# A hybrid attention and convolution block on one core: score maxima one step later, the second norm's factor in one tile, and a last row block in two halves

## The chip, the core and the metric

The kernel runs on one core of one Trainium2 chip. A core has TensorE (matmuls; the profile calls it PE, its weight loads PEld), VectorE (DVE), ScalarE (ACT), GpSimd (POOL) and SyncE (SP), each with an instruction stream of its own that runs in order. The metric is the device time of one execution in microseconds (us), as the median of several runs. A profiled execution gives the trace: its span is the time from the first to the last instruction, and its own device time is a little longer.

## The reference

One layer on 256 tokens of width 2048, everything in float32:

```python
xn = rms_norm(h, norm1_g)
q, k, v, ga, gg = split(xn @ w_in)            # 4 heads, 2 score maps each, d = 128
q, k = rope(rms_norm(q)), rope(rms_norm(k))
p = softmax(q @ k.T * scale, masked by chunks of 64)   # for both maps
att = rms_norm((p[0] - lam * p[1]) @ v) * (1 - lambda_init)
u = silu(layer_norm(causal_depthwise_conv(ga * sigmoid(gg))))
h = h + concat(att, u) @ w_out
hn = rms_norm(h, norm2_g)
h = h + (silu(hn @ w_gate) * (hn @ w_up)) @ w_down     # hidden width 5632
```

## The kernel before

The tokens are two row blocks of 128 (`NM = 2`, index `m`). Every float32 weight tile is split on the chip into a rounded part (`whi`, cast on ScalarE at L325) and a remainder (`wlo`, subtracted on VectorE at L334, or made by an accumulating DMA); a product is then three fp32r matmuls: data-high by weight-high, data-low by weight-high (L364 and L365 in the projections, L1066 and L1067 in the feed-forward part), data-high by weight-low (L370, L1072).

The projections run as chunks of two 128-row slices of a weight against 512 columns: eight matmuls in a first half, four in a second (`multiply`, L340 on). Everything else is written as Python generators that run beside the chunks: `resume()`, called after each half chunk, lets every running generator go on to its next `yield`, and what it issues then stands at that place in each engine's stream. So `lag(n)` puts the next step n half chunks later. This, and nothing at run time, sets the order. On VectorE the taps of the depthwise convolution (L553, `y`) fill in between, as many per chunk as a running credit of time allows (`run_side`).

Attention, per head (`attend_scores`): TensorE makes the scores (`ps_s`, L692), VectorE masks them and takes the row maxima (L700 to L704, `nmx`), ScalarE the exponentials (L714, `pr`), VectorE the combined weights (L728, `wt`), TensorE transposes these (L736 to L738, `ps_wt`), ScalarE copies them out (L741). Per head again (`attend_values`): TensorE makes the output (`ps_o`, L762), ScalarE sums squares, GpSimd makes the norm's factor (L769, L770, `ro`), ScalarE scales (L774, `att`), TensorE transposes (L782, `ps_at`), ScalarE and VectorE split the result (L786 `mahi`, L789 `malo`). Heads 0 and 1 reach their scores near 162 us, heads 2 and 3 near 211 us, when the values of heads 0 and 1 are also on their way.

After the output projection, `out_done` sums the squares of each row block of `h` (L462) into `ss2[m]`. For the last quarter it reduces them and makes the factor `rstd2[m]` with `rsqrt_mean` (L222 and L223, on GpSimd: scale and add, then a power of -0.5), once for each row block. `make_forms` spreads these factors along rows: ScalarE writes `rep` (L953), TensorE transposes it (`ps_r`, L957), ScalarE copies it to `rb` (L960).

The feed-forward part uses sums of quarter matrices (seven products where eight blocks would be multiplied, PSUM banks `q0` to `q7`; `Q1` to `QX` are their numbers). Plain chunks are of kind "g" or "u" (`multiply_two`); a "u" chunk adds into bank Q3 for row block 0 and bank QX for row block 1. The last chunk of the program runs row block 0 whole, then row block 1 whole. `down_whole` then adds bank and residual (`hend[m]`, already holding the other terms) on VectorE in halves of 256 columns (L1220), and SP stores each half as it is ready (L1221). An earlier store of the block before leaves on GpSimd's queue (L1202).

Of the kernel before, what the change touches and what calls it, by code (L numbers as in the profile page):

```python
# [18 lines left out]
P = 128  # L19
D = 2048  # L20
# [107 lines left out]
def tile_block(  # L128
# [554 lines left out]
    def attend_scores(hd):  # L683
        scs = []
        yield
        yield from room(2, 2)
        for m in range(NM):
            L = (m + 1) * P
            sc = aux_ps.tile([P, 2, S], F32, tag="aux", name="ps_s")
            for c in range(2):  # L690
                g = 2 * hd + c
                pe.matmul(sc[:, c, :L], qkT["q"][:, g, m * P : (m + 1) * P], qkT["k"][:, g, :L],  # L692
                          start=True, stop=True)
            scs.append(sc)
        yield from lag(2)
        nmxs, fs, prs, sms = [], [], [], []
        for m in range(NM):
            L = (m + 1) * P
            sc = scs[m]
            dve.memset(sc[:CHUNK, :, L - CHUNK : L], MASKED)  # L700
            nmx = small.tile([P, 2], F32, tag="nmx", name="nmx")
            dve.tensor_reduce(nmx, sc[:, :, :L], AX.X, ALU.max, negate=True)
            f = fqs[hd // 2, m][:, hd % 2 * 2 : hd % 2 * 2 + 2]
            dve.tensor_tensor(nmx, nmx, f, ALU.mult)  # L704
            nmxs.append(nmx)
            fs.append(f)
        spend(0.1)
        yield from lag(3)
        for m in range(NM):
            L = (m + 1) * P  # L710
            pr = pre.tile([P, 2, S], F32, tag="pr", name="pr", bufs=4)
            sm = small.tile([P, 2], F32, tag="sm", name="sm")
            for c in range(2):
                act.activation(pr[:, c, :L], scs[m][:, c, :L], AF.Exp, bias=nmxs[m][:, c : c + 1],  # L714
                               scale=fs[m][:, c : c + 1], accum_out=sm[:, c : c + 1])
            prs.append(pr)
            sms.append(sm)
        held[0] -= 2
        yield from lag(2)
        wts = []  # L720
        for m in range(NM):
            L = (m + 1) * P
            r = small.tile([P, 1], F32, tag="r", name="r")
            c = small.tile([P, 1], F32, tag="a1", name="c")
            dve.reciprocal(r, sms[m][:, 1:2])
            dve.scalar_tensor_tensor(c, sms[m][:, 0:1], neg_lam, r, ALU.mult, ALU.mult)
            wt = pre.tile([P, S], F32, tag="wt", name="wt", bufs=4)
            dve.scalar_tensor_tensor(wt[:, :L], prs[m][:, 1, :L], c, prs[m][:, 0, :L], ALU.mult, ALU.add)  # L728
            pool.tensor_scalar(eps_s[:, hd, m : m + 1], sms[m][:, 0:1], sms[m][:, 0:1], EPS, ALU.mult, ALU.mult)
            wts.append(wt)  # L730
        spend(0.3)
        spend(0.4)
        yield from lag(4)
        yield from room(1)
        pt = aux_ps.tile([P, 3, P], F32, tag="aux", name="ps_wt")
        pe.transpose(pt[:, 0, :], wts[0][:, :P], ident)  # L736
        pe.transpose(pt[:, 1, :], wts[1][:, :P], ident)
        pe.transpose(pt[:, 2, :], wts[1][:, P:], ident)  # L738

        wT = qkT["q"][:, 2 * hd : 2 * hd + 2, :].rearrange("p g s -> p (g s)")[:, : 3 * P].rearrange("p (k s) -> p k s", k=3)  # L740
        act.copy(wT, pt)  # L741
        wTs[hd] = wT
# [51 lines left out]

    hn = []
    ss2 = [const.tile([P, 4], F32, tag=f"ss2_{m}", name=f"ss2_{m}") for m in range(NM)]
    rstd2 = [const.tile([P, 1], F32, tag=f"rstd2_{m}", name=f"rstd2_{m}") for m in range(NM)]

    def out_done(n, ps):
        cs = slice(n * N, (n + 1) * N)  # L800
        for m in range(NM):
            dve.tensor_tensor(h[m][:, cs], h[m][:, cs], ps[m], ALU.add)
        if n == 2:
            held[0] -= NM
        yield
        for t in range(0, N // P, 2):
            k = n * (N // P) + t
            yield from room(1)
            pt = aux_ps.tile([P, 2, S], F32, tag="aux", name="ps_h")
            for i in range(2):  # L810
                for m in range(NM):
                    pe.transpose(pt[:, i, m * P : (m + 1) * P], h[m][:, (k + i) * P : (k + i + 1) * P], ident)
            if k % HK == 0:
                hn.append(early.tile([P, HK, S], F32, tag="wb", name="hn"))
            rows = hn[k // HK][:, k % HK : k % HK + 2, :]
            for i in range(2):
                act.activation(rows[:, i, :], pt[:, i, :], AF.Copy, scale=col("g2", k + i))
            hi, lo = lhs_two("h", k)
            act.copy(hi, rows)
            dve.tensor_tensor(lo, rows, hi.bitcast(F32), ALU.subtract)  # L820
            for i in range(2):
                hT[k + i] = (hi[:, i, :], lo[:, i, :])
            yield
        for m in range(NM):
            square_sum(h[m][:, cs], ss2[m][:, n : n + 1])
            pool.dma_start(out=hd[m][:, cs], in_=h[m][:, cs])
        if n == D // N - 1:
            yield
            for m in range(NM):
                ss = small.tile([P, 1], F32, tag="ssh", name="ssh")  # L830
                dve.tensor_reduce(ss, ss2[m], AX.X, ALU.add)
                rsqrt_mean(rstd2[m], ss, D, EPS)
            yield
            yield
            prestack.close()
            ffn["pool"] = ctx.enter_context(tc.tile_pool(name="ffn", bufs=1))
            start(make_forms())
# [216 lines left out]
    def multiply_two(c):  # L1054
        hi, lo = c["hi"], c["lo"]
        qs = (Q3, QX) if c["kind"] == "u" else (Q2, Q4)
        xs = []
        for k in c["ks"]:
            while (x := c["plain"](k)) is None:
                resume()  # L1060
            xs.append(x)

        def first_half(m):
            ms = slice(m * P, (m + 1) * P)
            ps = sum_bank(c, qs[m])
            pe.matmul(ps, xs[i][0][:, ms], hi[:, i, :], start=i == 0 and bool(c["first"].get(qs[m])), stop=False)  # L1066
            pe.matmul(ps, xs[i][1][:, ms], hi[:, i, :], start=False, stop=False)  # L1067

        def second_half(m):
            ms = slice(m * P, (m + 1) * P)  # L1070
            for i in range(2):
                pe.matmul(sum_bank(c, qs[m]), xs[i][0][:, ms], lo[:, i, :], start=False,  # L1072
                          stop=i == 1 and bool(c["last"].get(qs[m])))

        if c is chunks[-1]:

            for m in range(NM):
                for i in range(2):
                    first_half(m)
                second_half(m)  # L1080
        else:
            for i in range(2):
                for m in range(NM):
                    first_half(m)
            resume()
            for m in range(NM):
                second_half(m)
        resume()
        if c["done"]:
            start(c["done"](c["sums"]))  # L1090
# [118 lines left out]
    def down_whole(g, n, q, end):  # L1209
        while "us" not in end:  # L1210
            yield
        us = end["us"]
        for m, i in enumerate((Q3, QX)):
            if not at_end(g, n):
                dve.tensor_tensor(us[m], q[i], us[m], ALU.add)
                continue
            w = N // 2
            for a in range(0, N, w):
                hs = hend[m][:, N + a : N + a + w]
                dve.tensor_tensor(hs, hs, q[i][:, a : a + w], ALU.add)  # L1220
                sp.dma_start(out=out[m * P : (m + 1) * P, (n + 1) * N + a : (n + 1) * N + a + w], in_=hs)  # L1221
        if not at_end(g, n):
            if FGROUPS[g] > 3:
                yield from lag(HD_LAG)
            for m in range(NM):
                pool.dma_start(out=hd[m][:, (n + 1) * N : (n + 2) * N], in_=us[m], accum_op=ALU.add)
        if g == len(FGROUPS) - 1 and not at_end(g, n):
            fetch_end()

            yield from lag(6)  # L1230
            for m in range(NM):
                cs = slice(n * N, (n + 2) * N)
                pool.dma_start(out=out[m * P : (m + 1) * P, cs], in_=hd[m][:, cs])
# [18 lines left out]
    for g, nb in enumerate(FGROUPS):  # L1252
# [7 lines left out]
            chunks[-1]["prompt"] = True  # L1260
        down_pass(g, j0, nb)
        j0 += nb

    near_pair = lambda t: any(c.get("kind") == "s" for c in chunks[t : t + HI_AHEAD + 1])
    lead = lambda t: (1, 1) if t < OPENING else (HI_AHEAD, LO_AHEAD) if near_pair(t) else (AHEAD, AHEAD)
# [46 lines left out]
```

## Time and profile before

| | |
|---|---|
| median of 3 runs | 1038.59 us (1038.37 to 1038.63) |
| profiled execution, device time | 1038.44 us |
| its span | 1036.7 us |
| granted TensorE clock | 1.00 |
| TensorE busy | 99% of the span |
| VectorE / ScalarE / GpSimd busy | 89% / 62% / 11% |
| last matmul ends | about 1032.6 us |

In a timeline a row gives the start in us, the duration in us, the engine, the source line, the operation, what it writes and reads, and in brackets how long its engine stood idle before it and for whom. `x4` means four such instructions merged into one row, whose duration then runs from the first one's start to the last one's end. Matmuls overlap: the next one starts before the row of the one before it ends, so distances are taken between starts. In a row of the waits stand the engine, the tile and line that waited, the one waited for, and then the total in us, the number of times and the longest. The windows view cuts the span into stretches and gives each engine's busy time in each.

### The profile page before, as it was taken

To read this page: it belongs to the slowest core of one execution; us is meant where nothing else is said; L and a number is where in the kernel's file an instruction comes from. 1 tells how busy PE (TensorE), PEld (TensorE's weight loads), DVE (VectorE), ACT (ScalarE), POOL (GpSimd) and SP (SyncE) were. 2 spreads that over 40 slices of the span, in tenths; PEclk is the share of its full clock that TensorE was granted. 3 is DMA by queue.
4 is the path that set the end of the run, shared out by engine and by line. 5 is a ranking of instruction groups with operands and counts; after the bars stand their busy time and mean duration, and the time that the engine had idled before them with its cause. 6 is when DMAs were issued, how large, how long until landed. Compare 5 with 4: busy or idle time off the path is not lost.

```text
span 1036.7 us, 13003 instructions
## 1 busy us (share of the span) xinstructions
PE 1028.9 (99%) x4639; PEld 848.7 (82%) x4639; DVE 926.5 (89%) x1125; ACT 638.3 (62%) x780; POOL 110.8 (11%) x149
## 2 busy tenths in 40 slices
PE   9999999999999999999999999999999999999998
PEld 7888888878888788888888888888888888888886
DVE  7899999989766599999999898989999989889887
ACT  7554657655666565777666556667757556667452
POOL 0130112111000100110102011101001111010010
PEclk9999999999999999999999999999999999999999
DMA  9657654553547677987989799879798979897773
GB/s 351 213 181 279 214 174 142 192 174 127 186 158 235 187 247 232 285 255 217 260 250 266 262 252 273 261 228 260 230 269 250 295 197 284 245 261 232 217 220 102
DMA packets 115664, 237.59 MB, mean 229 GB/s; under 512 B 7696, under 2 KB 8848, under 8 KB 115344
## 3 DMA queue, kind: packets, MB, share of 16 engines
q1 hardware_dynamic: 104864, 203.71, 58.7%
q0 software_dynamic: 10592, 33.04, 16.5%
q8 instruction: 36, 0.59, 0.2%
q14 instruction: 28, 0.23, 0.1%
q10 hardware_dynamic: 144, 0.03, 0.0%
HBM read 204.24 MB, written 9.44 MB: 206 GB/s over the span
## 4 chain that ended last, share of the span: by engine, by line
PE 63%; DVE 2%; issue 1%; ACT 0%; DVEq 0%
PE q L1066 11%; PE q L1067 11%; PE q L1072 11%; PE q L1047 9%; PE q L1045 9%; PE q L1046 9%; PE ps_a L870 1%; PE acc L370 1%; PE acc L364 1%; PE acc L365 1%; DVE wlo L334 1%; DVE wlt L1028 0%; DVE wt L1018 0%; DVE wt L1019 0%; ACT wh L1024 0%
## 5 line engine op out<-in xcount | busy, mean ns | idle before, releaser
L325 ACT CAST whi<-raw 128x1024 fp32r<-128x1024 f32 (+1 forms) x257 | 266.4, 1047 | 151.4 <-PE acc L365 82.0
L334 DVE TENSOR_TENSOR wlo<-raw,whi 128x1024 fp32r<-128x1024 f32 (+1 forms) x211 | 254.4, 1217 | 37.5 <-ACT whi L325 37.3
L1024 ACT CAST wh<-wt 128x2048 fp32r<-128x2048 f32 x60 | 114.9, 1915 | 108.3 <-DVE wt L1020 108.2
L1028 DVE TENSOR_TENSOR wlt<-wt,wh 128x2048 fp32r<-128x2048 f32 x60 | 137.5, 2291 | 19.5 <-ACT wh L1024 19.4
L364 PE MATMUL acc<-whi,xhi 128*128 128x512 f32 x320 | 127.2, 397 | 0.9 <-ACT whi L325 0.9
L365 PE MATMUL acc<-whi,xlo 128*128 128x512 f32 x320 | 125.3, 392 | 0.0
L1066 PE MATMUL q<-whi,chi 128*128 128x512 f32 x320 | 125.3, 391 | 0.0
L1067 PE MATMUL q<-whi,clo 128*128 128x512 f32 x320 | 124.6, 389 | 0.0
L1045 PE MATMUL q<-wh,fhi 128*128 128x512 f32 x280 | 109.9, 392 | 0.0
L1046 PE MATMUL q<-wh,flo 128*128 128x512 f32 x280 | 109.0, 389 | 0.0
L1027 DVE TENSOR_TENSOR wlb<-wb,wh 128x1536 fp32r<-128x1536 f32 x60 | 105.1, 1752 | 1.1 <-ACT wh L1021 1.1
L553 DVE SCALAR_TENSOR_TENSOR y<-upad,cw,y 128x256 f32<-128x256 f32 x240 | 101.9, 481 | 2.2 <-ACT y L546 2.2
L329 POOL DMA_DIRECT2D wlo<-raw x46 | 40.2, 875 | 507.9 <-ACT wlo L328 244.6
L1021 ACT CAST wh<-wb 128x1536 fp32r<-128x1536 f32 x60 | 88.4, 1473 | 0.0
L370 PE MATMUL acc<-wlo,xhi 128*128 128x512 f32 x320 | 87.4, 394 | 0.0
L1072 PE MATMUL q<-wlo,chi 128*128 128x512 f32 x320 | 85.6, 389 | 0.0
L1066 PE MATMUL q<-whi,ahi 128*128 128x512 f32 x192 | 74.9, 390 | 0.0
L1067 PE MATMUL q<-whi,alo 128*128 128x512 f32 x192 | 74.8, 389 | 0.0
L1018 DVE TENSOR_TENSOR wt<-wb 128x1024 f32<-128x1024 f32 x60 | 73.1, 1219 | 0.0
L364 PEld LDWEIGHTS acc<-whi,xhi 128*128 128x128 f32 x320 | 60.4, 189 | 14.3 <-ACT whi L325 1.7
L365 PEld LDWEIGHTS acc<-whi,xlo 128*128 128x128 f32 x320 | 60.4, 189 | 12.6
L1072 PEld LDWEIGHTS q<-wlo,chi 128*128 128x128 f32 x320 | 59.9, 188 | 12.8 <-DMA wlo<-raw 0.2
(245 smaller groups left out, 1833.9 us busy)
## 6 DMA issues: line engine op xcount, KB each, us to landing
raw<-in_w_in_dram SPq DMA_DIRECT2D x79, 512.0 KB, 4.6
raw<-in_w_gate_dram SPq DMA_DIRECT2D x48, 512.0 KB, 5.2
raw<-in_w_up_dram SPq DMA_DIRECT2D x48, 512.0 KB, 5.3
raw<-in_w_down_dram SPq DMA_DIRECT2D x48, 512.0 KB, 6.8
wlo<-raw POOLq DMA_DIRECT2D x46, 512.0 KB, 7.2
wb<-in_w_up_dram SPq DMA_DIRECT2D x40, 512.0 KB, 4.4
wb<-in_w_gate_dram SPq DMA_DIRECT2D x40, 512.0 KB, 5.5
wb<-in_w_down_dram SPq DMA_DIRECT2D x40, 512.0 KB, 6.0
```

The source lines that it names most:

```text
L325: act.copy(c["hi"], c["raw"])
L334: dve.tensor_tensor(c["lo"], c["raw"], c["hi"].bitcast(F32), ALU.subtract)
L364: pe.matmul(ps[m], xhi[:, ms], hi[:, j, :], start=c["first"] and j == 0, stop=False)
L365: pe.matmul(ps[m], xlo[:, ms], hi[:, j, :], start=False, stop=False)
L1024: act.copy(c["hi"][:, :SUMMED], c["t"])
L1027: dve.tensor_tensor(lob, c["b"][:, 1:], c["hi"][:, SUMMED:].bitcast(F32), ALU.subtract)
L1028: dve.tensor_tensor(lot, c["t"], c["hi"][:, :SUMMED].bitcast(F32), ALU.subtract)
L1045: pe.matmul(ps, hi, c["hi"][:, w], start=bool(first), stop=False)
L1046: pe.matmul(ps, lo, c["hi"][:, w], start=False, stop=False)
L1066: pe.matmul(ps, xs[i][0][:, ms], hi[:, i, :], start=i == 0 and bool(c["first"].get(qs[m])), stop=False)
L1067: pe.matmul(ps, xs[i][1][:, ms], hi[:, i, :], start=False, stop=False)
L1072: pe.matmul(sum_bank(c, qs[m]), xs[i][0][:, ms], lo[:, i, :], start=False, stop=i == 1 and bool(c["last"].get(qs[m])))
```

## The change

Three separate edits. First, the step of `attend_scores` that masks the scores and takes their maxima is queued three half chunks after the scores instead of two; all later steps of that head follow it. Second, the reduced sums of squares and the factor of the second norm become one tile of 128x2 for both row blocks, so `rsqrt_mean` is called once. Third, in the last chunk of the program row block 1 no longer adds into bank QX: bank QX is closed one chunk earlier and added to `hend[1]` by a new generator, `last_row_but_one`, and the last chunk's share of row block 1 goes, 256 columns at a time, into two fresh PSUM tiles (`qe`); the very last store is issued by ScalarE.

```diff
-        yield from lag(2)
+        yield from lag(3)
         nmxs, fs, prs, sms = [], [], [], []
...
-    rstd2 = [const.tile([P, 1], F32, tag=f"rstd2_{m}", name=f"rstd2_{m}") for m in range(NM)]
+    rstd2s = const.tile([P, NM], F32, tag="rstd2", name="rstd2")
+    rstd2 = [rstd2s[:, m : m + 1] for m in range(NM)]
...
+            ss = small.tile([P, NM], F32, tag="ssh", name="ssh")
             for m in range(NM):
-                ss = small.tile([P, 1], F32, tag="ssh", name="ssh")
-                dve.tensor_reduce(ss, ss2[m], AX.X, ALU.add)
-                rsqrt_mean(rstd2[m], ss, D, EPS)
+                dve.tensor_reduce(ss[:, m : m + 1], ss2[m], AX.X, ALU.add)
+            rsqrt_mean(rstd2s, ss, D, EPS)
...
         if c is chunks[-1]:
-            for m in range(NM):
+            for i in range(2):
+                first_half(0)
+            second_half(0)
+            c["sums"]["ends"] = []
+            for a in range(0, N, N // 2):
+                cs = slice(a, a + N // 2)
+                ps = acc_ps.tile([P, N], F32, tag="acc", name=f"qe{a}")[:, : N // 2]
                 for i in range(2):
-                    first_half(m)
-                second_half(m)
+                    xhi, xlo = (x[:, P:] for x in xs[i])
+                    pe.matmul(ps, xhi, hi[:, i, cs], start=i == 0, stop=False)
+                    pe.matmul(ps, xlo, hi[:, i, cs], start=False, stop=False)
+                for i in range(2):
+                    pe.matmul(ps, xs[i][0][:, P:], lo[:, i, cs], start=False, stop=i == 1)
+                c["sums"]["ends"].append(ps)
...
-                dve.tensor_tensor(hs, hs, q[i][:, a : a + w], ALU.add)
-                sp.dma_start(out=out[m * P : (m + 1) * P, (n + 1) * N + a : (n + 1) * N + a + w], in_=hs)
+                dve.tensor_tensor(hs, hs, q["ends"][a // w] if m else q[i][:, a : a + w], ALU.add)
+                (act if m and a else sp).dma_start(
+                    out=out[m * P : (m + 1) * P, (n + 1) * N + a : (n + 1) * N + a + w], in_=hs)
...
+    def last_row_but_one(q):
+        yield
+        dve.tensor_tensor(hend[1][:, N:], hend[1][:, N:], q[QX], ALU.add)
+    before_last = [c for c in chunks if c.get("kind") == "u"][-2]
+    before_last["last"][QX] = True
+    before_last["done"] = lambda q: last_row_but_one(q)
```

ScalarE's stream where heads 0 and 1 are scaled (`att`) and head 3's exponentials are taken (`pr`); the lines with a sign are those that moved:

```order
 L462 ACTIVATE junk,sso<-ps_o 128x256 x4
 L325 CAST whi<-raw 128x1024
+L774 ACTIVATE att<-ps_o,ro 128x256 x2
 L714 ACTIVATE pr,sm<-ps_s,nmx,fq 128x128 x2
 L714 ACTIVATE pr,sm<-ps_s,nmx,fq 128x256 x2
-L774 ACTIVATE att<-ps_o,ro 128x256 x2
 L786 ACTIVATE mahi<-ps_at,cols 128x256 x2
 L774 ACTIVATE att<-ps_o,ro 128x256 x2
 L325 CAST whi<-raw 128x1024
```

Head 0's scaling now stands ahead of head 3's exponentials, and these stand between it and head 1's scaling.

TensorE's stream a chunk later, before:

```order
L365 MATMUL acc<-whi,xlo_242 128x512
L736 MATMUL ps_wt<-ident,wt 128x128
L737 MATMUL ps_wt<-ident,wt 128x128
L738 MATMUL ps_wt<-ident,wt 128x128
L782 MATMUL ps_at<-ident,att 128x128 x4
L370 MATMUL acc<-wlo,xhi_241 128x512 x4
L364 MATMUL acc<-whi,xhi_265 128x512
```

and now:

```order
L365 MATMUL acc<-whi,xlo_241 128x512
L782 MATMUL ps_at<-ident,att 128x128 x4
L370 MATMUL acc<-wlo,xhi_240 128x512 x4
L736 MATMUL ps_wt<-ident,wt 128x128
L737 MATMUL ps_wt<-ident,wt 128x128
L738 MATMUL ps_wt<-ident,wt 128x128
L364 MATMUL acc<-whi,xhi_264 128x512
```

The transposes of head 2's weights have moved behind the second half of the chunk; the transposes of head 1's output come straight after its first half. The other three heads' weight transposes move past one second half in the same way.

The end of VectorE's stream, before:

```order
L1206 TENSOR_TENSOR hend<-hend,sum_8739 128x512
L1220 TENSOR_TENSOR hend<-hend,q_8680 128x256 x2
L1220 TENSOR_TENSOR hend<-hend,q_8729 128x256 x2
```

and now, where L1217 is the old L1206, L1231 the old L1220 and L1278 the new generator:

```order
L1217 TENSOR_TENSOR hend<-hend,sum_8734 128x512
L1278 TENSOR_TENSOR hend<-hend,q_8724 128x512
L1231 TENSOR_TENSOR hend<-hend,q_8675 128x256 x2
L1231 TENSOR_TENSOR hend<-hend,qe_8786 128x256
L1231 TENSOR_TENSOR hend<-hend,qe_8793 128x256
```

One sum of 512 columns is added, and the last two sums read a tile each instead of the two halves of one bank.

More of the change, by code (lines that the diff above doesn't have):

```diff
@@ L1262, in tile_block @@
         j0 += nb
+    def last_row_but_one(q):
+        yield
+        dve.tensor_tensor(hend[1][:, N:], hend[1][:, N:], q[QX], ALU.add)
+    before_last = [c for c in chunks if c.get("kind") == "u"][-2]
+    assert before_last["done"] is None
+    before_last["last"][QX] = True
+    before_last["done"] = lambda q: last_row_but_one(q)
     near_pair = lambda t: any(c.get("kind") == "s" for c in chunks[t : t + HI_AHEAD + 1])
```

## The prediction

> **What bounds the kernel now.** I read the page first (span, busy times), then the waits of TensorE alone, then the timeline at the three places that the diff touches.
>
> ```profile
> span 1036.7 us, 13003 instructions
> PE 1028.9 (99%) x4639; PEld 848.7 (82%) x4639; DVE 926.5 (89%) x1125; ACT 638.3 (62%) x780; POOL 110.8 (11%) x149
> ```
>
> TensorE is busy for all but 7.8 us. So a change that takes no matmul away can win only what TensorE idles, and the stretch after its last matmul. The waits of TensorE itself (us in total, times, longest) show where that is:
>
> ```profile
> PE ps_at L782 <- ACT att L774: 0.8, 1, 0.8
> PE ps_r L957 <- ACT rep L953: 0.3, 1, 0.3
> ```
>
> These are two places, both in the change: the transposes of the attention output (`ps_at`) and of the second norm's factor (`ps_r`). A matmul's row reaches past the start of the next, so the rows understate what is lost; I take each stall from start to start below. The third place is the end, where the chain leaves TensorE for VectorE and the stores.
>
> **Part one, the maxima a half chunk later.** The stall, on TensorE, and the same sequence without a wait 26 us later:
>
> ```profile
> 229.35 1.07 PE L370 MATMUL acc<-wlo,xhi 128*128 128x512 f32 x4
> 231.18 0.91 PE L782 MATMUL ps_at<-ident,att 128*128 128x128 f32 x4 [0.77 <-ACT att L774]
> 231.84 0.48 PE L364 MATMUL acc<-whi,xhi 128*128 128x512 f32 x1
> ...
> 256.65 1.07 PE L370 MATMUL acc<-wlo,mahi 128*128 128x512 f32 x4
> 257.56 0.60 PE L782 MATMUL ps_at<-ident,att 128*128 128x128 f32 x4
> 257.92 0.48 PE L364 MATMUL acc<-whi,mahi 128*128 128x512 f32 x1
> ```
>
> Undisturbed, the matmul behind the transposes starts 257.92 - 256.65 = 1.27 us after the `L370` group; here it took 231.84 - 229.35 = 2.49. The stall is 1.22 us. ScalarE shows why:
>
> ```profile
> 228.68 0.46 ACT L714 ACTIVATE pr<-ps_s,nmx,fq 128x128 f32<-128x128 f32 x1
> ...
> 230.64 0.85 ACT L774 ACTIVATE att<-ps_o,ro 128x256 f32<-128x256 f32 x2
> 232.13 0.84 ACT L786 ACTIVATE mahi<-ps_at,cols 128x256 fp32r<-128x256 f32 x2 [0.64 <-PE ps_at L782]
> 232.85 0.84 ACT L774 ACTIVATE att<-ps_o,ro 128x256 f32<-128x256 f32 x2
> ```
>
> Head 0's scaling (`L774`) stands behind head 3's exponentials (`L714`), which hold ScalarE for 230.64 - 228.68 = 1.96 us. The new order puts the scaling first. Its factor is there in time: the second of two such powers on GpSimd, head 1's, started at 228.19, so head 0's was done before.
>
> ```profile
> 228.19 0.70 POOL L770 TENSOR_TENSOR ro<-sso,neghalf 128x2 f32<-128x2 f32 x1
> ```
>
> So head 0's scaling starts at 228.68 instead of 230.64, the transposes find their input, and TensorE goes on at 229.35 + 1.27 = 230.62.
>
> Not all of that stays. The exponentials now stand ahead of head 1's scaling. A pair on ScalarE takes 0.72 us (232.13 to 232.85): head 0's scaling from 228.68, exponentials from 229.40, `mahi` from 231.36, head 1's scaling from 232.08. Before, `L364` started 231.84 - 230.64 = 1.20 us after the scaling that it waited for; so TensorE gets past head 1's transposes at 233.28. It would be ready for that earlier:
>
> ```profile
> 233.78 0.27 PE L736 MATMUL ps_wt<-ident,wt 128*128 128x128 f32 x1
> ...
> 234.11 0.60 PE L782 MATMUL ps_at<-ident,att 128*128 128x128 f32 x4
> 234.47 1.17 PE L370 MATMUL acc<-wlo,xhi 128*128 128x512 f32 x4
> 235.47 0.39 PE L364 MATMUL acc<-whi,xhi 128*128 128x512 f32 x1
> ```
>
> Eight matmuls take 233.78 - 231.84 = 1.94 us, the transposes 0.36, so 230.62 + 1.94 + 0.36 = 232.92. The stall returns as 0.36 us, since head 2's weight transposes (`L736`, 0.33 us), which stood between and covered it, have moved behind the `L370` group. That separate batch also costs a changeover: `L370` to `L364` took 1.00 us behind transposes and 0.91 without (256.65 to 257.56), so 0.09. Part one is worth 1.22 - 0.36 - 0.09 = 0.77 us. From both sides: 1.22 if nothing returns; a loss if the lateness of the maxima reaches TensorE elsewhere (a rival below).
>
> What else is queued behind the moved maxima? On VectorE three taps and a `wlo` subtraction now go ahead of them; that `wlo` waits for a cast:
>
> ```profile
> 213.13 0.17 DVE L700 MEMSET ps_s<- 64x128 f32 x1
> 215.47 1.27 DVE L553 SCALAR_TENSOR_TENSOR y<-upad,cw,y 128x256 f32<-128x256 f32 x3
> 214.65 1.05 ACT L325 CAST whi<-raw 128x1024 fp32r<-128x1024 f32 x1 [3.02 <-PE acc L365]
> 228.81 1.22 DVE L334 TENSOR_TENSOR wlo<-raw,whi 128x1024 fp32r<-128x1024 f32 x1 [1.58 <-ACT whi L325]
> ```
>
> From 213.13, where head 2's maxima began, the taps' 1.27 us bring VectorE to 214.4, the cast ends at 215.7, and everything behind runs up to 1.3 us late, until the pause of 1.58 us before 228.81 absorbs it. The weight transposes that need the maxima also move later, by the `L370` group's 0.91 us. I price this at nothing; without that cover it is the fourth rival.
>
> **Part two, the norm's factor in one tile.** Two POOL operations on 128x2 replace four on 128x1:
>
> ```profile
> 351.70 1.15 POOL L222 TENSOR_SCALAR rsq<-ssh 128x1 f32<-128x1 f32 x1 [7.38 <-DVE ssh L831]
> 352.93 0.57 POOL L223 TENSOR_TENSOR rstd<-rsq,neghalf 128x1 f32<-128x1 f32 x1
> 354.46 0.69 ACT L953 ACTIVATE rep<-ident,rstd 128x128 f32<-128x128 f32 x2 [3.23 <-POOL rstd L223]
> 354.21 0.39 PE L365 MATMUL acc<-whi,hlo 128*128 128x512 f32 x1
> 354.91 0.62 PE L957 MATMUL ps_r<-ident,rep 128*128 128x128 f32 x2 [0.32 <-ACT rep L953]
> 355.29 1.17 PE L370 MATMUL acc<-wlo,hhi 128*128 128x512 f32 x4
> ```
>
> A 512-column matmul takes 0.227 us from start to start (four in the 0.91 above), so TensorE was free at 354.44; a 128-column transpose takes 0.11 (233.78 to 234.11 for three). Unstalled, `L370` would start at 354.44 + 0.22 = 354.66; it started at 355.29. The stall is 0.63 us. Now the power runs once, on 128x2, for 0.70 us (the `L770` row): ready at 352.93 + 0.70 = 353.63, both `rep` done by 353.67 + 0.69 = 354.36, before TensorE asks at 354.44. Worth 0.63; at worst nothing: the first factor was ready at 353.5, and both `rep` waited for the second, up to 354.46, which is one operation with the first now. The first POOL operation, 1.15 us, I leave as it is.
>
> **Part three, the end.** The last row block ran in six 512-column matmuls, then two VectorE halves, then two stores on SP:
>
> ```profile
> 1031.98 0.61 PE L1072 MATMUL q<-wlo,ahi 128*128 128x512 f32 x2
> 1032.63 0.42 DVE hend L1220
> 1033.08 0.81 SPq L1221 DMA_DIRECT2D out_dram<-hend  x2
> L1221 SPq DMA_DIRECT2D out_dram<-hend x4: 332/360/385, 1031.7 to 1033.5; - x4
> DMA to landing us min/median/max: 1.9/1.9/1.9
> ```
>
> The last store was issued at 1033.5, 0.9 us after TensorE's end at 1032.6: behind both halves and the other store. Now only one half is behind the last matmul: 0.02 to its start, 0.42 for it (the chain's step), and 0.03 to the issue (1033.05 to 1033.08), 0.47 us. That gains 0.43. The added sum of bank QX, 128x512, at most two such halves long (0.84), can start when the chunk before is done, and lies beside the first row block's six matmuls (1.36).
>
> Against it: twelve 256-column matmuls for six of 512. No such fp32r form stands in the trace. Bounds: half the time each, 12 x 0.113 = 1.36, as before; no shorter, 12 x 0.227 = 2.72, 1.36 more. Nearest rows:
>
> ```profile
> 162.34 1.47 PE L692 MATMUL ps_s<-kT,qT 128*128 128x128 f32 x8
> L692 PEld LDWEIGHTS ps_s<-kT,qT x32: 187/190/192, 162.1 to 219.0; 128*128 128x128 f32 x32
> DMA to landing us min/median/max: 2.5/2.5/2.5
> ```
>
> Eight score passes (fp32, 128 and 256 columns), each with a weight load of its own, take 1.47 us from the first start to the last end. At one load's 0.19 each, seven starts and even the shortest pass (0.27, `ps_wt`) would be 1.60. So a load shown as 0.19 us does not hold the pace at 0.19, and I take 0.12 a half: 1.44, 0.08 more. The end is worth 0.43 - 0.08 = 0.35; bounds 0.43 and -0.93.
>
> The last store moves to ScalarE's queue. SP, with its third store issued by about 1032.9, would be free as well, so I price the queue at nothing. ScalarE's only transfer before, the load of `cols` at the start, landed after 2.5 us (the fence's last row) instead of 1.9; that is the bound, 0.6 lost. The Trainium skill (DMA: Bandwidth & Descriptors, Rules for kernel authors) says that stores spread over SP, ScalarE and GpSimd run on the same 16 DMA engines, and that only issue time of the sequencer is saved; that speaks against this edit and would leave the sum as it is. The skill's TensorE: Matmul & The Clock Gate (Back-to-back issue gap) gives 262 cycles at 256 columns, 0.109 us, by which the halves would cost 1.31 and the end gain 0.48; the trace's 512-column step, 0.227, is longer than the page's 0.216, so I keep 0.12.
>
> **Sum.** 0.77 + 0.63 + 0.35 = 1.75 us off the profiled execution's 1038.44 (span 1036.7 plus 1.7 around it) is 1036.7. The three timed runs have 1038.59, 0.15 more: 1036.8, which is 0.17% below.
>
> **Rivals.**
> 1. *Nothing returns.* Head 1's scaling is early enough, or other work fills the place: 1.22 + 0.63 + 0.43 = 2.3, so 1036.3. For it: part of my 0.36 rests on 0.1 us differences between three engines. Against it: 1.96 us of exponentials must go somewhere ahead of `mahi`.
> 2. *The halves are no shorter.* Weight loads set the pace: 1.36 lost against 0.43 gained, 0.77 + 0.63 - 0.93 = 0.47, so 1038.1. For it: a load's row is 0.19, longer than half a matmul. Against it: the score rows above.
> 3. *The change does not do what it says.* TensorE finds its next wait at the same places (the factor of head 0 late, `rep` held by something else), and the end alone pays: 1038.59 - 0.35 = 1038.2. Against it: the waits name their releasers.
> 4. *Slower.* A later maximum delays exponentials, weights and their transposes, and TensorE, in order, stands at each head's `ps_wt`. A half chunk's 1.36 us (six matmuls) for each of four heads is 5.4 us, with 0.98 won at the other places: 1038.59 + 5.4 - 0.98 = 1043.0. It decides from where the weights come later than the moved group's 0.91 plus their lead.
>
> ```profile
> 237.67 0.48 DVE L728 SCALAR_TENSOR_TENSOR wt<-pr,c 128x256 f32<-128x256 f32 x1
> 240.03 0.28 PE L736 MATMUL ps_wt<-ident,wt 128*128 128x128 f32 x1
> ```
>
> Head 3's weights end at 238.15 and TensorE takes them at 240.03, a lead of 1.9. So the weights would have to be 2.8 us late; the 1.3 above is the most that I find.
>
> **How the numbers follow.** 0.2%, about what a measurement of this kernel can tell from no change, is 2.08 us: faster means below 1036.5, slower above 1040.7. My forecast: 0.52, its own range 1036.2 to 1037.5, a quarter of it (0.14) below 1036.5. Rival 1: 0.18, all faster. Rival 2: 0.10, rival 3: 0.12, both within. Rival 4: 0.08. So faster 0.32, the same 0.60, slower 0.08. The 8-in-10 range goes from 1035.9 (rival 1 with a little more) to 1038.7 (rivals 2 and 3 with some loss), leaving out rival 4 and some of each tail.
>
> **What would show it.** In the new profile: no wait of `ps_at` on ScalarE near 230, one of 0.3 to 0.4 us some 2 us later; `att` ahead of `pr` on ScalarE; `ps_r` without a wait, the second `rep` ready before TensorE asks; 256-column matmuls 0.12 us apart; the last store issued 0.5 us after the last matmul and landed 1.9 us later. A wait at `ps_wt`, or VectorE idle for more than about 1.5 us between 160 and 228, would prove me wrong.

## The result and the profile after

| | before | changed |
|---|---|---|
| median of 13 runs each, us | 1038.63 (1037.83 to 1039.57) | 1036.39 (1035.99 to 1036.94) |
| span of the profiled execution, us | 1036.7 | 1034.2 |

The ratio is 0.9978, with a 95% interval of 0.9971 to 0.9986: 2.24 us less, with room from 1.45 to 3.0. That is just past the 0.2% (2.08 us) that the prediction took as the bound of what can be told from no change, and the interval lies on both sides of it. The page of the changed kernel:

```profile
span 1034.2 us, 13010 instructions
PE 1028.1 (99%) x4645; PEld 848.9 (82%) x4645; DVE 927.3 (90%) x1126; ACT 638.3 (62%) x780; POOL 108.7 (11%) x147
```

Of the 2.5 us by which the span is shorter, TensorE's busy time makes 0.8; the rest is idle time and the stretch behind the last matmul. The waits of TensorE, all but the one for the warm-up at the start (total, times, longest, in us):

```profile
PE acc L364 <- ACT whi L325: 0.6, 1, 0.6
PE q L1048 <- DVE wlt L1029: 0.2, 1, 0.2
```

Neither `ps_at` nor `ps_r` is among them. The waits of its weight loads do still have one for the attention's scaling. The first row is the kernel before, the second the changed one:

```profile
PEld ps_at L782 <- ACT att L774: 1.6, 3, 1.2
PEld ps_at L782 <- ACT att L774: 0.8, 3, 0.4
```

**Part one.** The same place on TensorE in the timeline of the changed kernel, and then on ScalarE:

```profile
229.11 1.07 PE L370 MATMUL acc<-wlo,xhi 128*128 128x512 f32 x4
230.02 0.60 PE L782 MATMUL ps_at<-ident,att 128*128 128x128 f32 x4
230.37 0.48 PE L364 MATMUL acc<-whi,xhi 128*128 128x512 f32 x1
...
232.08 0.40 PE L365 MATMUL acc<-whi,xlo 128*128 128x512 f32 x1
232.41 0.91 PE L782 MATMUL ps_at<-ident,att 128*128 128x128 f32 x4
233.07 1.19 PE L370 MATMUL acc<-wlo,xhi 128*128 128x512 f32 x4
...
234.35 0.48 PE L364 MATMUL acc<-whi,xhi 128*128 128x512 f32 x1
234.66 0.39 PE L365 MATMUL acc<-whi,xlo 128*128 128x512 f32 x1
```

```profile
228.44 0.84 ACT L774 ACTIVATE att<-ps_o,ro 128x256 f32<-128x256 f32 x2
...
231.12 0.87 ACT L786 ACTIVATE mahi<-ps_at,cols 128x256 fp32r<-128x256 f32 x2
231.83 0.88 ACT L774 ACTIVATE att<-ps_o,ro 128x256 f32<-128x256 f32 x2
```

`L370` to the `L364` behind the first transposes is 1.26 us now (230.37 - 229.11), where it was 2.49: the whole stall of 1.23 is gone. The second transposes now wait: TensorE could have begun them at 232.31 and gone on at 232.67, but `L370` starts at 233.07, 0.40 later. They need head 1's scaling, which runs from 231.83 to 232.71 behind the exponentials. By 234.66 the net gain is 0.80 us: that matmul stood at 235.70 before, so it is 1.04 earlier, of which 0.24 was there at 229.11 already. On VectorE the pause of 1.58 us before 228.81 is down to 0.39, so it did absorb the lateness of what stands behind the maxima.

**Part two.** GpSimd and TensorE at the second norm, in two timelines:

```profile
350.70 1.09 POOL L222 TENSOR_SCALAR rsq<-ssh 128x2 f32<-128x2 f32 x1 [7.43 <-DVE ssh L832]
351.88 0.71 POOL L223 TENSOR_TENSOR rstd<-rsq,neghalf 128x2 f32<-128x2 f32 x1
```

```profile
353.13 0.39 PE L365 MATMUL acc<-whi,hlo 128*128 128x512 f32 x1
353.37 0.38 PE L958 MATMUL ps_r<-ident,rep 128*128 128x128 f32 x2
353.50 1.17 PE L370 MATMUL acc<-wlo,hhi 128*128 128x512 f32 x4
```

The transposes start 0.24 us behind the matmul ahead of them, without a wait. `L365` stood at 354.21 before and `L370` at 355.29, so they are 1.08 and 1.79 earlier: 0.71 from this place.

**Part three.** The end, on TensorE, VectorE and ScalarE's queue:

```profile
1028.99 0.28 PE L1087 MATMUL qe<-whi,ahi 128*128 128x256 f32 x1
1029.11 0.28 PE L1088 MATMUL qe<-whi,alo 128*128 128x256 f32 x1
...
1029.23 0.19 PEld L1088 LDWEIGHTS qe<-whi,alo 128*128 128x128 f32 x1
...
1030.18 0.40 PE L1090 MATMUL qe<-wlo,ahi 128*128 128x256 f32 x2
1030.62 0.42 DVE L1231 TENSOR_TENSOR hend<-hend,qe 128x256 f32<-128x256 f32 x1 [0.30 <-PE qe L1090]
1031.07 0.36 ACTq L1232 DMA_DIRECT2D out_dram<-hend  x1
```

The 256-column matmuls stand 0.119 us apart (1028.99 to 1030.18 are ten steps) although each load of weights still shows 0.19. From the first matmul of the last row block to the last store's issue it is now 1031.07 - 1028.99 = 2.08 us, where it was 1033.5 - 1031.07 = 2.43 (the first of the six matmuls started at 1031.07): 0.35 less. Up to the last VectorE half it is 0.07 longer (1.63 against 1.56), from there to the issue 0.42 shorter (0.45 against 0.87).

The three places make 0.80 + 0.71 + 0.35 = 1.86. The spans differ by 2.5; some 0.24 of the rest lies ahead of all three places and 0.29 between 355 and 1029 us, where TensorE's lead over the kernel before grows from 1.79 to 2.08. Whether these two belong to the change was the first question for the experiments.

### The profile page after: what moved, and what is told of

Read it like the earlier page. It is cut to its first block, busy times and chain, and to the rows that moved or that the text cites. A ratio compares the mean times of both kernels' runs of the same rounds, so it can differ in the third digit from the quotient of the medians.

```text
span 1034.2 us, 13010 instructions
## 1 busy us (share of the span) xinstructions
PE 1028.1 (99%) x4645; PEld 848.9 (82%) x4645; DVE 927.3 (90%) x1126; ACT 638.3 (62%) x780; POOL 108.7 (11%) x147
## 4 chain that ended last, share of the span: by engine, by line
PE 96%; DVE 2%; DMA 1%; issue 1%; ACT 0%; SPq 0%; DVEq 0%
PE acc L364 11%; PE acc L365 11%; PE acc L370 11%; PE q L1067 11%; PE q L1068 11%; PE q L1073 11%; PE q L1048 9%; PE q L1046 9%; PE q L1047 9%; PE ps_a L871 1%; DVE wlo L334 1%; DMA raw<-in_w_in_dram 1%; PE ps_s L692 1%; PE ps_o L762 1%; DVE wlt L1029 0%
## 5 line engine op out<-in xcount | busy, mean ns | idle before, releaser
L364 PE MATMUL acc<-whi,xhi 128*128 128x512 f32 x320 | 127.2, 398 | 0.7 <-ACT whi L325 0.6
L365 PE MATMUL acc<-whi,xlo 128*128 128x512 f32 x320 | 125.1, 391 | 0.0
L370 PE MATMUL acc<-wlo,xhi 128*128 128x512 f32 x320 | 87.1, 393 | 0.0
L364 PEld LDWEIGHTS acc<-whi,xhi 128*128 128x128 f32 x320 | 60.3, 189 | 14.5 <-ACT whi L325 2.0
L365 PEld LDWEIGHTS acc<-whi,xlo 128*128 128x128 f32 x320 | 60.3, 188 | 12.3
```

The source lines that it names most:

```text
L364: pe.matmul(ps[m], xhi[:, ms], hi[:, j, :], start=c["first"] and j == 0, stop=False)
L365: pe.matmul(ps[m], xlo[:, ms], hi[:, j, :], start=False, stop=False)
L370: pe.matmul(ps[m], xhi[:, ms], lo[:, j, :], start=False, stop=c["last"] and j == nk - 1)
```

## The experiments

Medians in us; the kernel before ran beside each group on the same chip.

| run | median | before | ratio, 95% interval |
|---|---|---|---|
| e1_maxima | 1037.77 | 1038.68 | 0.9980 to 0.9998 |
| e2_norm | 1037.44 | 1038.68 | 0.9979 to 0.9997 |
| r_norm (again) | 1037.82 | 1038.78 | 0.9981 to 0.9998 |
| e3_end | 1038.23 | 1038.68 | 0.9988 to 1.0005 |
| e4_store_sp | 1036.56 | 1038.68 | 0.9971 to 0.9988 |
| f1_head3 | 1036.27 | 1038.62 | 0.9972 to 0.9990 |
| r_head3 (again) | 1036.17 | 1038.78 | 0.9967 to 0.9986 |
| f2_exps | 1036.45 | 1038.62 | 0.9972 to 0.9990 |
| f3_lag6 | 1038.36 | 1038.62 | 0.9993 to 1.0011 |
| f4_whole | 1036.72 | 1038.62 | 0.9973 to 0.9990 |
| g_uneven | 1035.99 | 1038.78 | 0.9966 to 0.9984 |
| r_before | 1038.49 | 1038.78 | 0.9989 to 1.0007 |

An interval is some 1.8 us wide, so parts of 0.4 us are read at their place in the trace; the medians only say whether the total agrees.

**Each part alone.** First the maxima:

```diff
-        yield from lag(2)
+        yield from lag(3)
         nmxs, fs, prs, sms = [], [], [], []
```

> The kernel before with only the maxima a half chunk later. Theory (the changed kernel's trace): the 1.23 us stall at the first ps_at goes, about 0.35 comes back at the second, so 0.9 us less, 1037.7 beside 1038.6. Rival, nothing comes back: 1.2 us less. Rival, the lateness of the maxima costs something elsewhere: less than 0.5. In the trace: the first ps_at without a wait, a wait of about 0.4 us at the second one.

Measured: 0.91 less by the medians. TensorE's timeline:

```profile
229.45 1.07 PE L370 MATMUL acc<-wlo,xhi 128*128 128x512 f32 x4
230.36 0.60 PE L782 MATMUL ps_at<-ident,att 128*128 128x128 f32 x4
...
232.74 0.91 PE L782 MATMUL ps_at<-ident,att 128*128 128x128 f32 x4
...
234.99 0.39 PE L365 MATMUL acc<-whi,xlo 128*128 128x512 f32 x1
```

From 0.10 late at `L370` to 0.71 early at `L365` (235.70 before): 0.81, as in the changed kernel. The second wait shows as the long row of 0.91 again, not as a wait of TensorE proper.

Then the factor in one tile (the two hunks of the diff at `rstd2` and `ssh`):

> The kernel before with only the second norm's factor in one 128x2 tile. Theory: the wait of ps_r on rep goes and nothing follows, 0.7 us less (0.63 in the prediction), 1037.9 beside 1038.6. Rival, TensorE finds a next wait soon after and gives it back: under 0.2 less. In the trace: no wait at ps_r, and the shift of TensorE's starts stays what it is from 356 us to the end.

Measured: 1.24 less by the medians, and 0.71 at its place: 0.57 early ahead of `ps_r` (353.64 against 354.21), 1.28 behind it (354.01 against 355.29). The wait is gone, and nothing follows it. The medians' surplus was taken up again below.

Then the end (the diff from `multiply_two` on):

> The kernel before with only the end changed: two 256-column halves, the sum of QX one chunk earlier, the last store on ScalarE. Theory: 0.4 us less (0.43 for the shorter way behind the last matmul, 0.0 to 0.08 given back by the halves), 1038.2. Rival, the slow drift of 0.3 us between 356 and 1027 us in the changed kernel's trace belongs to the change of the end: 0.7 less. If neither this run's trace nor the two others show that drift with a sign of their own part, it is the spread between runs.

Measured: 0.45 less by the medians, an interval that reaches past 1. In its trace the last row block starts at 1032.07 and the last store is issued at 1034.16, 2.09 us, as in the changed kernel (2.08). So the parts alone show 0.81, 0.71 and 0.34 at their places, 1.86 in all: together they neither help nor hinder each other there.

The drift between 355 and 1029 us was not the end's: this trace drifted the other way, by 0.67 us. The rows that go with it are waits of TensorE's weight loads for an accumulating DMA. For the kernel before, for `e3_end` and for a run below (`r_norm`):

```profile
PEld q L1072 <- DMA wlo<-raw: 0.2, 1, 0.2
```

```profile
PEld q L1072 <- DMA wlo<-raw: 1.0, 2, 0.5
```

```profile
PEld q L1073 <- DMA wlo<-raw: 0.7, 1, 0.7
```

The changed kernel has no such row and drifts by -0.29 against the kernel before; `e3_end` with 1.0 of it drifts by +0.67, `r_norm` with 0.7 by +0.26, `e2_norm` with none by -0.26. A remainder that comes late in one execution makes that trace longer. It does not explain the whole -0.29: the kernel before had only 0.2 of such waits, and its second trace, without any, is just 0.10 shorter there (the table under "What is spread").

**Which queue for the last store.**

```diff
-                (act if m and a else sp).dma_start(
+                sp.dma_start(
```

> The changed kernel with its last store on SP again, nothing else. Theory of the prediction (queue priced at 0): the same as the changed kernel within 0.1 us, 2.2 less than before; SP has issued its third store before the last half is added. Rival, each issue holds SP for some 0.4 us and the last one waits behind the third: up to 0.4 us longer than the changed kernel. Rival, ScalarE's queue lands a store later (2.5 against 1.9): up to 0.6 us shorter.

Measured: 2.12 less than before, against 2.24 for the changed kernel: the same. SP's four issues take 1.80 us from 1029.92, up to 1031.72, and the last one starts at 1031.3, when its VectorE half ends (1030.90 + 0.42 = 1031.32). SP is free when it is needed, and the last store lands after 1.9 us from either queue, so neither rival holds.

**Head 3 alone.**

```diff
-        yield from lag(3)
+        yield from lag(3 if hd == 3 else 2)
         nmxs, fs, prs, sms = [], [], [], []
```

> The changed kernel, but only head 3's maxima come a half chunk later; heads 0 to 2 keep the old lag. Theory: the stall at the first ps_at is head 3's exponentials alone, so it stays away; and head 2's weight transposes stand between the two heads' attention transposes again, which covers what came back (0.40 us) and saves the changeover of the separate batch. So 0.4 us less than the changed kernel, 1036.0. Rival, the other heads' lag also mattered: the same as the changed kernel, or longer by up to 0.9 if the stall returns. In the trace: the first L364 behind the second ps_at starts some 0.4 us less after the first ps_at than in the changed kernel (234.35 - 230.02 = 4.33 there, with the weight transposes in both).

TensorE's timeline of this kernel:

```profile
229.32 1.07 PE L370 MATMUL acc<-wlo,xhi 128*128 128x512 f32 x4
230.24 0.60 PE L782 MATMUL ps_at<-ident,att 128*128 128x128 f32 x4
...
232.52 0.27 PE L736 MATMUL ps_wt<-ident,wt 128*128 128x128 f32 x1
...
232.85 0.69 PE L782 MATMUL ps_at<-ident,att 128*128 128x128 f32 x4
233.29 1.17 PE L370 MATMUL acc<-wlo,xhi 128*128 128x512 f32 x4
...
242.85 0.39 PE L364 MATMUL acc<-whi,mahi 128*128 128x512 f32 x1
```

The stall stays away, so it was head 3's exponentials alone, and head 2's weight transposes (`ps_wt`) fill the place where TensorE waited for head 1. Against the kernel before this place is worth 1.16 us: 0.03 early at 229.32, and 1.19 early at the first product of the attention output (`mahi`), which started at 244.04 before. In the changed kernel that product starts at 243.00, 1.04 early with 0.24 at the outset, 0.80: the difference is 0.36. The median is only 0.12 lower; the run was repeated:

> Head 3's maxima alone later (with the other two parts), a second time: the trace showed 0.37 us less around the attention than in the changed kernel, the median 0.12 less. Theory: 0.37 is its worth: some 2.5 us less than the kernel before over both sets. Rival, it is lost again later: 2.2, as the changed kernel.

Measured: 1036.17, 2.61 less than before, and 1.17 at the place (0.67 early at 228.68, 1.84 at 242.20). The worth in the trace is settled; that the kernel is faster than the changed one by 0.36 is what the traces say and the medians (0.12 and 0.22 lower) do not contradict.

**Head 3's exponentials later still**, on top of the change:

```diff
         spend(0.1)
-        yield from lag(3)
+        yield from lag(4 if hd == 3 else 3)
         for m in range(NM):
```

> The changed kernel with head 3's exponentials one more half chunk later, so that ScalarE scales head 1 ahead of them. Theory: what came back at the second ps_at was the exponentials' 1.96 us on ScalarE; now the second ps_at finds its input, 0.4 us less than the changed kernel, 1036.0. Rival, the exponentials' lateness is only moved on: TensorE waits at head 3's weight transposes or at head 1's cast mahi behind them, 0.3 us or more longer than the changed kernel.

TensorE's timeline:

```profile
232.59 0.62 PE L782 MATMUL ps_at<-ident,att 128*128 128x128 f32 x4
232.97 1.17 PE L370 MATMUL acc<-wlo,xhi 128*128 128x512 f32 x4
...
241.60 0.27 PE L736 MATMUL ps_wt<-ident,wt 128*128 128x128 f32 x1
242.20 0.33 PE L737 MATMUL ps_wt<-ident,wt 128*128 128x128 f32 x1 [0.33 <-DVE wt L728]
```

The wait at the second transposes goes: `L370` to `L370` is 3.58 us, against 233.07 - 229.11 = 3.96 in the changed kernel, 0.38 less. It is lost 9 us later, where head 3's weights are late for their transposes: 0.60 from `L736` to `L737` instead of 0.11. From `L370` at 229.39 to the first product with `mahi` at 243.40 it is 14.01 us, against 243.00 - 229.11 = 13.89: 0.12 worse. The median is 0.06 above the changed kernel's. The theory was right on the wait at the second transposes and wrong on the total; the rival named the right place, at less than its price of 0.3 or more.

**The maxima of all heads three half chunks later still**, lag 6:

> The changed kernel with the maxima of all heads three more half chunks later (lag 6 instead of 3). Theory of the prediction's fourth rival: lateness of the maxima reaches TensorE at each head's weight transposes, a half chunk's 1.4 us or more for each, 4 us or more longer than the changed kernel. Theory from the order: everything behind the maxima in a head's own sequence moves with them, the weight transposes too, so no wait appears there; the change is within 1 us, and comes from which of ScalarE's jobs stand ahead of the attention's scaling.

Measured: seven executions took 1037.7 to 1038.4 us, three 1040.1 to 1040.7; the profiled one is of the three. No wait at `ps_wt` in it. The wait is elsewhere, where the convolution's result enters:

```profile
280.47 0.60 PE L611 MATMUL ps_ln<-ident,upad 128*128 128x128 f32 x4
282.76 0.49 PE L364 MATMUL acc<-whi,mchi 128*128 128x512 f32 x1 [1.70 <-DVE mchi L618]
...
283.72 0.63 PE L364 MATMUL acc<-whi,mchi 128*128 128x512 f32 x1
284.14 0.63 PE L365 MATMUL acc<-whi,mclo 128*128 128x512 f32 x1
```

Its windows, with the granted clock in the column after the engines:

```profile
279.50:282.70 3.20, 1.56 (x9) 1.08 (x8) 1.51 (x2) 3.20 (x6) 0.00 (x0) 1.00 0.10 38
282.70:286.50 3.80, 3.74 (x10) 2.69 (x11) 2.26 (x5) 1.07 (x2) 0.00 (x0) 0.59 0.39 138
```

Both theories missed the place. The weight transposes did move along with the maxima, so nothing waits there, but the convolution's own norm slid against the matmuls that read it, and TensorE stood for it. On top the granted clock fell to 0.59 behind that wait. The median is 2.0 us above the changed kernel's, the three long executions 3.7 to 4.3. No trace of the shorter seven was taken, so it stays open whether they were spared the slow clock. A wait of this length need not bring it: in `e1_maxima` TensorE had one of 1.71 us near its start, and from 8.3 to 11.7 us its granted clock was 1.00, its 512-column matmuls 0.23 us apart (8.70, 8.93, 9.16).

```profile
8.36 0.50 PE L364 MATMUL acc<-whi,xhi 128*128 128x512 f32 x1 [1.71 <-ACT whi L325]
```

**The last row block undivided.** Six 512-column matmuls into one new bank, both VectorE halves from it:

```diff
-            for a in range(0, N, N // 2):
-                cs = slice(a, a + N // 2)
-                ps = acc_ps.tile([P, N], F32, tag="acc", name=f"qe{a}")[:, : N // 2]
+            ps = acc_ps.tile([P, N], F32, tag="acc", name="qe")
...
+            for a in range(0, N, N // 2):
+                c["sums"]["ends"].append(ps[:, a : a + N // 2])
```

> The changed kernel with its last row block in six 512-column matmuls again, into one new bank; the early sum of QX, the two VectorE halves and the last store on ScalarE stay. Theory: TensorE's last row block is 0.07 us shorter (six at 0.227 against twelve at 0.119), both VectorE halves come behind the last matmul, 0.36 to 0.42 more: 0.3 us longer than the changed kernel, 1036.7. Rival, the second half is not what the end waits for: no difference. In the trace: 0.4 us more from TensorE's end to the last store's issue.

The end of this kernel:

```profile
1029.20 0.39 PE L1085 MATMUL qe<-whi,ahi 128*128 128x512 f32 x1
...
1030.10 0.61 PE L1088 MATMUL qe<-wlo,ahi 128*128 128x512 f32 x2
1030.76 0.75 DVE L1230 TENSOR_TENSOR hend<-hend,qe 128x256 f32<-128x256 f32 x2 [0.61 <-PE qe L1088]
1031.54 0.35 ACTq L1231 DMA_DIRECT2D out_dram<-hend  x1
```

From the block's first matmul to the last issue: 2.34 us, against 1031.07 - 1028.99 = 2.08 with halves. So the halves are worth 0.26, and the median is 0.33 above the changed kernel's, as expected. The early sum of QX and ScalarE's queue by themselves leave little: 2.34 against 1033.5 - 1031.07 = 2.43 before.

**The last row block as 384 and 128 columns**, on top of `f1_head3`:

```diff
+    EDGES = (0, 384), (384, 512)
...
-            for a in range(0, N, N // 2):
-                cs = slice(a, a + N // 2)
+            for a, b in EDGES:
+                cs = slice(a, b)
...
```

The sums and the stores of this row block are divided at the same column.

> The same with the last row block in 384 and 128 columns instead of two 256. Theory, TensorE's time goes by columns: six at 0.17 and six at 0.06, no longer than now, and the last VectorE sum of 128 columns is some 0.1 us shorter: 0.1 less. Rival, a 128-column fp32r matmul is no shorter than its weight load's pace (0.11 in the transposes, or more): 0.3 us or more for the six, 0.2 or more longer.

The matmuls of the narrow piece:

```profile
1030.02 0.22 PE L1089 MATMUL qe<-whi,ahi 128*128 128x128 f32 x1
1030.08 0.27 PE L1090 MATMUL qe<-whi,alo 128*128 128x128 f32 x1
1030.19 0.27 PE L1089 MATMUL qe<-whi,ahi 128*128 128x128 f32 x1
```

128 columns take 0.11 us a step, hardly less than the 0.119 of 256 columns. From the block's first matmul (1028.95) to the last issue (1031.15) it is 2.20 us, 0.12 more than with equal halves. This is the rival's mechanism, at less than its price. Its median, 1035.99, is the lowest of all, but 0.18 from `r_head3` is within the spread, and the trace gives the end no reason to be better.

**What is spread.** The kernel before and the factor alone once more:

> The kernel before, unchanged, as if it were an experiment. Theory: the parts of the traces' shift that lie ahead of the changed places (the first weights' arrival, the fourth weight slice taken at 9.88 us there and at 9.42 to 10.53 in the others) and the drift behind them are the spread of single executions: this trace differs from the first one of the same kernel by some 0.2 to 0.5 us there too, and the medians of two sets of runs of one kernel by 0.2 us or less. Rival, they belong to the kernels: this trace repeats the first within 0.1 us.

> The factor in one tile alone, a second time: its first timing came out 1.2 us below the kernel before, where its own place in the trace shows 0.70. Theory: the place is worth 0.70 and the rest is spread, so this time 0.5 to 1.0 less than before. Rival, it has a second gain that its trace shows elsewhere: 1.2 less again, and its fourth weight slice again some 0.4 us earlier than the others'.

The kernel before against itself: 0.29 less by the medians, an interval of -0.11% to +0.07%. Its trace follows the first one within 0.07 up to 356 us and within 0.17 at the end, so those two agree better than my theory had it. The arrival of the first weights does differ between traces of one kernel: the factor alone took its fourth weight slice at 9.42 us in the first run and at 9.90 in the second, `f1_head3` at 10.02 and `r_head3` at 9.40. Of the 0.24 by which the changed kernel led at 229 us, 0.12 was there at the `L370` group near 14.6 us (14.61 before, 14.49 now). That half is spread.

The other half is not, and neither is the whole drift behind the norm. The table has two distances between starts on TensorE: from that `L370` group to the one ahead of the first `ps_at`, near 229 us, and from the first `L364` behind `ps_r` (356.30 in the kernel before) to the `L1072` pair that closes row block 0 of the last chunk (1030.62). The last column is what the weight loads waited for the accumulating DMA.

| trace | 14.6 to 229 us | 356 to 1030 us | waits for the DMA |
|---|---|---|---|
| kernel before | 214.74 | 674.32 | 0.2 |
| r_before | 214.73 | 674.22 | none |
| e3_end | 214.73 | 674.99 | 1.0 |
| e1_maxima | 214.61 | 674.60 | 0.5 |
| e2_norm | 214.62 | 674.06 | none |
| r_norm | 214.60 | 674.58 | 0.7 |
| changed kernel | 214.62 | 674.03 | none |

On the first stretch the three traces without the later maxima and without the factor in one tile agree to 0.01, and all others but `f3_lag6`, whose order differs, are some 0.12 shorter (the six that are not in the table: 214.59 to 214.63). On the second, among traces without a wait for the DMA, those with the factor in one tile are shorter than `r_before` by 0.16 to 0.23. So about 0.12 + 0.19 = 0.31 us of the changed kernel's gain builds up at none of the three places, and it repeats from trace to trace. Here the rival of `r_before`, that such shifts belong to the kernels, is right, though not within the 0.1 it named. In `e2_norm` the program ahead of 340 us issues the same work in the same order as before, so the order of the work does not make it there; what does is not shown.

For the factor, the second timing is 0.96 less, and its place shows 0.71 (0.20 early at `L365`, 0.91 at the `L370` behind the transposes). Both medians lie above the place; their intervals (0.2 to 2.2) hold 0.7. The rival of `r_norm`, a second gain elsewhere, has the table on its side: 0.12 and 0.16 in the first trace of the factor alone, which brings 0.71 to about 1.0. The fourth weight slice has no part in it.

## Why the prediction came out as it did

It said 1036.8 us; 1036.4 was measured, inside its range. Point by point:

- *The stall of 1.22 us at the first transposes* went whole (1.23). Its cause, head 3's exponentials ahead of head 0's scaling, is shown by `f1_head3`, where only that head is later.
- *What returns.* 0.36 for the wait at head 1 and 0.09 for the changeover were forecast; 0.40 of wait was measured, and 0.43 in all, so the changeover came to 0.03. Part one was 0.77 in the sum and is 0.80 (0.81 alone). `f2_exps` shows that head 3's exponentials ahead of head 1's scaling made the wait (with them behind it, 0.38 of the 0.40 goes), and `f1_head3` that head 2's transposes in between cover it: 1.16 of the stall stays won. The first rival, that nothing returns, is out, though its 1036.3 is nearer to the measured time than the forecast's 1036.8: the time alone would have picked the wrong mechanism.
- *The maxima queued a half chunk later, priced at nothing.* Right: no wait at `ps_wt`, and no second idle time on VectorE of the size named as a sign of error. The lead of head 3's weights over their transposes fell from 1.9 to 1.16 us (238.75 to 239.91). The margin was thin: `f2_exps` meets the fourth rival's wait at head 3's weights with one half chunk more for their exponentials, at 0.5 us for one head and not 1.36 for each of four; with lag 6 the bill comes somewhere that no rival named.
- *The factor in one tile, 0.63.* Mechanism right, size short: 0.71 in three traces. The term of the sum that was off is the 0.22 us for two transposes; here `L370` follows them after 353.50 - 353.37 = 0.13, so the unstalled start was earlier and the stall larger than I had it.
- *The end, 0.35.* 0.35 from the block's first matmul to the last issue, as 0.42 behind the last matmul less 0.07 for the halves, where the sum had 0.43 and 0.08. The 0.12 a half was right (0.119), and with it the second rival fell; but the score passes only spoke against a pace of 0.19, so that it came out at 0.12 and not between the two was in part luck. The queue's price of nothing was right (`e4_store_sp`).

The places make 1.86 where I had 1.75, and the medians 2.24. Most of what lies between is the 0.31 that builds up along the program. The prediction held that a change which takes no matmul away can win only what TensorE idles and the stretch behind its last matmul, and its sum has no term for this gain; the runs show the gain and not its cause. The rest is well within the ratio's interval. The chances put "within 0.2%" (0.60) ahead of "faster" (0.32); the bound stood at 2.08, and the places alone lie short of it, the measured median just past it.

## What to carry to other kernels

When a step is queued later to let another pass on an in-order engine, follow the step that was overtaken to its next consumer: here 0.4 of 1.2 us came back a chunk later, and moving only the one head that stood in the way kept it, since other heads' transposes then filled the gap. Where a tail is a sum behind the last matmul, halve the last tile's width only down to where a matmul step still shrinks: 0.227, 0.119 and 0.11 us at 512, 256 and 128 columns. And price gains of a few tenths from starts at their place in the trace, not from spans, since the first weights' arrival alone moved the spans of one kernel by 0.5 us. Then compare the stretches in between as well, with a second trace of the kernel before beside them: a distance that repeats to 0.01 in one kernel and differs by 0.12 in another is not spread.

## What the runs showed of the hardware that was not expected

- TensorE's clock fell behind a short wait: in `f3_lag6` TensorE had no matmul for about 1.7 us, and the following 3.8 us ran at a granted 0.59, with matmuls 0.43 us apart instead of 0.227. The stall of 1.22 us at the first `ps_at` of the kernel before cost no clock. Nor did the wait of 1.71 us near the start of `e1_maxima`. So the length of the wait alone does not decide it, and one trace does not show what does. The Trainium skill (TensorE: Matmul & The Clock Gate, What's actually happening) has the clock drop to half after at least one idle window of about 3.4 us; here a wait of half that length was followed by it.
- A 128-column fp32r matmul with a weight load of its own takes 0.11 us a step, the same as a 128-column transpose, while 256 columns take 0.119: below 256 columns the step hardly shrinks.
